# Projecting the values of all heads in a stage of their own, by one level of Strassen's algorithm, and reading them back per pair of heads

## The chip, the cores and the metric

The kernel runs on one core of a Trainium2 chip. The metric is the device time of one execution in microseconds (us). The kernel before takes 1388.06 us (median of 3 runs, 1387.71 to 1388.27). The profile is of one execution that took 1388.24 us, of which its span covers 1386.5 us.

The engines are named as in the profile: PE is the tensor engine (PEld its weight loads), DVE the vector engine, ACT the scalar engine, POOL the GpSimd engine, and SP the queue that issues every DMA. Each takes its instructions in a fixed order.

## The reference, cut to what matters

One decoder block over x of 512 tokens by 1024 features, in float32: a gated feed-forward layer with layer norm, then a mixer, a second layer norm, and a second feed-forward layer with layer norm. The part that the change touches is in the mixer.

```
proj = h @ w_in + b_in                       # h: 512 x 1024
q, k, v, g, glu_a, glu_b, gate_r, gate_c = split(proj)
q, k = rotary(q) * 128 ** -0.5, rotary(k)    # 8 heads of 128
v = v.reshape(8 heads of 256)                # v: 512 x 2048
scores = (q k^T) * decay_mask; r = scores @ v; r = per-head norm of r
ret_out = (silu(g) * r) @ w_ret_o
u = glu_a * sigmoid(glu_b); u = causal convolution of u, 31 taps per channel
```

## The kernel before, in words

Every float32 operand of a product is split into a high part, rounded to the type fp32r (a cast on ACT), and a low part, the difference (a subtraction on DVE). A product is three matmuls: high by high, high by low, low by high (`split`, L64 to L66, and `mm3`).

The two feed-forward layers use one level of Strassen's algorithm: seven products of half-size blocks in place of eight, with sums of blocks of the weights and of x made by DVE. In them x is the moving operand. The sums of x are made by the steps f1 to f4 of `strassen_x` (L127 in the profile).

The mixer starts when the first layer norm has written its result, as features by tokens, into `xh` and `xl` (high and low part). The end of the first layer already projects two units of weights of 1 MB, for q and k of head 0 and for channel block 0 of the convolution (`qk_glu`). Then four pairs of heads follow. For one pair:

- `v_half`, twice: the values of both heads, 512 tokens by 512 columns. A half is one 1 MB unit of weights and 48 matmuls with 512 columns, with x stationary (L701 to L703). The four results stay in PSUM until `v_out` adds the bias (L712) and splits them.
- `scores` of a head, `retain` (scores by values, the norm's statistics, `rn` on ACT at L780) and `gated` (eight transposes of `rn` at L789, multiplied by the gate).
- in between, units of 48 matmuls with 512 columns (`unit_proj`): q and k of the next head (`qk_proj`), the gate of a head (`g_unit`), a block of the convolution's input (`glu`).

The taps of the convolution run on DVE (L328), some after each unit (`TAPS_HEAD`, `TAPS_LATE`). In the mixer the order on each engine is set by a planner from the written order, by its own costs; in the feed-forward layers it is the written order (`manual_schedule`). A tile of a pool with one buffer is written again only when its last reader is done.

The names that the change and the steps of the prediction touch:

```
raw = wpool.tile([P, 2048], ..., bufs=2)     # one unit of weights, 1 MB, loaded by SP
whi, wlo: 4 buffers of [P, 1024]             # its high and low parts, two buffers per unit
def unit_proj(src, taps): load, split, 2 x 24 matmuls of 512 columns, then conv_some(taps)
```

Of the kernel before, what the change touches and what calls it, by code (L numbers as in the profile page):

```python
# [8 lines left out]
F32 = mybir.dt.float32  # L9
F32R = mybir.dt.float32r  # L10
# [5 lines left out]
P = 128  # L16
# [10 lines left out]
ALPHA = 2.0 ** 0.25  # L27
KR = 4
WARM = 18
TAPS_HEAD = 5  # L30
TAPS_LATE = 9
HS = S // 2
KH = KD // 2
N_STD = (2, 3)
# [18 lines left out]
def block_kernel(ctx, tc, ap, out):  # L53
# [7 lines left out]
    def bank():  # L61
        return psum.tile([P, S], F32, name="ps", tag="ps")
# [247 lines left out]
    def vcol(i):  # L310
        return vec[:, i:i + 1]
# [288 lines left out]
    def first_unit(h):  # L600
# [25 lines left out]
        nc.sync.dma_start(vec, ap["vec"])  # L626
        return [ps0]

    w_in = ap["w_in"]
    qk_glu = ffn(ap["w1gu"], ap["w1dn"], ap["x"], 0, scratch1, N_STD[0], first_unit, first_parts, (w_in[U_QK], w_in[U_L]))  # L630


    with ExitStack() as mix:
        mp = mix.enter_context(tc.tile_pool(name="mix", bufs=1))

        def spare_z(shape, dtype):
            return mp.tile(shape, dtype, name="z", tag="z", bufs=17)

        def tok(dtype=F32):
            return spare_z([P, S], dtype)  # L640

        def chan(dtype=F32):
            return mp.tile([P, S], dtype, name="cv", tag="cv", bufs=KD + 1)


        mp.tile([P, PAD + S], F32, name="up", bufs=5)
        mp.tile([P, 32], F32, name="gap")
        tok()
        cv = [chan() for _ in range(KD)]

        def gate_unit(i, pool, sc):
            ps = unit_proj(w_in[U_R + i], TAPS_LATE)
# [6 lines left out]
        with tc.tile_pool(name="heads", bufs=1) as hp_:  # L659
            cs = hp_.tile([P, 2, S], F32, name="cs")  # L660
            nc.sync.dma_start(cs, ap["cs"])

            def glu(i, ps=None):
                ps = ps or unit_proj(w_in[U_L + i], TAPS_HEAD)
                sgb = hp_.tile([P, S], F32, name="sgb", tag="t1", bufs=2)
                nc.scalar.activation(sgb, ps[0], AF.Sigmoid, bias=vcol(C_BIN + T_B + i))
                up = mp.tile([P, PAD + S], F32, name="up", bufs=5)
                nc.gpsimd.memset(up[:, :PAD], 0.0)
                nc.vector.scalar_tensor_tensor(up[:, PAD:], ps[1], vcol(C_BIN + T_A + i), sgb, op0=ALU.add, op1=ALU.mult)
                conv_todo.append(conv_taps(cv[i], up, i))  # L670

            def qk_proj(h, ps=None):

# [15 lines left out]
                    r.append((rh, rl))  # L689
                return r  # L690

            def v_half(hp, kk, vps):
                ws = load_unit(w_in[U_V + 2 * hp + kk])
                for k4 in range(4):
                    k = kk * 4 + k4
                    wh, wl = ws[k4 // 2]
                    csl = slice((k4 % 2) * 512, (k4 % 2) * 512 + 512)
                    for st in range(ST):
                        o = vps[st]
                        ssl = slice(st * P, (st + 1) * P)  # L700
                        mm(o, xh[:, k, ssl], wh[:, csl], start=(k == 0), stop=False)  # L701
                        mm(o, xh[:, k, ssl], wl[:, csl], start=False, stop=False)  # L702
                        mm(o, xl[:, k, ssl], wh[:, csl], start=False, stop=(k == KD - 1))  # L703

            def v_out(hp, vps):

                bv = hp_.tile([P, 512], F32, name="bv")
                nc.sync.dma_start(bv, ap["b_v"][hp:hp + 1, :].partition_broadcast(P))
# [85 lines left out]
            glus = iter(range(KD))  # L794
# [24 lines left out]

        gp = mix.enter_context(tc.tile_pool(name="gates", bufs=1))  # L820
# [85 lines left out]
    def split_parts(h):  # L906
        def parts(i, j):
            sl = (slice(None), slice(i * KH, (i + 1) * KH), slice(j * HS, (j + 1) * HS))
            return [(slice(0, KH), [p.bitcast(F32)[sl] for p in (xh, xl)])]

        return parts

    ffn(ap["w2gu"], ap["w2dn"], scratch2, 4, out, N_STD[1], lambda h: started, split_parts, ())


# [82 lines left out]
```

## Time and profile before

| | |
|---|---|
| median of 3 runs | 1388.06 us |
| profiled execution | 1388.24 us |
| its span | 1386.5 us |
| PE busy | 1371.2 us, 99% |
| DVE busy | 995.3 us, 72% |
| ACT busy | 597.5 us, 43% |
| the four pairs of heads | 383.6 to 772.2 us of the span |

A duration in the profile is from the start of an instruction to its end. Instructions on one engine overlap a little, so what an instruction costs in a queue is the distance from its start to the next start. A matmul of 512 columns is shown with 0.39 us but the next starts 0.23 us later.

### The profile page before, as it was taken

Reading aid. Unit: us, or ns where it says so; the run is one execution under the profiler, and the core shown is the slowest. Engines: PE = TensorE matmul, PEld = TensorE weight load, DVE = VectorE, ACT = ScalarE, POOL = GpSimd, SP = SyncE. Lnnn points to the kernel's source line nnn. Section 1 sums busy time; section 2 is a strip of 40 time slices with the busy share of each in tenths; the row PEclk is TensorE's granted clock in tenths of the full one; section 3 lists DMA queues with packets and bytes.
Section 4 is the critical chain, followed back from the end, with each engine's and each line's share of the span. In section 5 each row is a group of like instructions: output and inputs, shape, how many; then the busy total and the mean of one; then the engine's idle time right before and its main releaser. Section 6 shows DMA issues by size and latency. Waiting matters only on the chain.

```text
span 1386.5 us, 19271 instructions
## 1 busy us (share of the span) xinstructions
PE 1371.2 (99%) x7974; PEld 1215.4 (88%) x7974; DVE 995.3 (72%) x1422; ACT 597.5 (43%) x872; POOL 21.8 (2%) x36
## 2 busy tenths in 40 slices
PE   9899999999999999999999999999999999999997
PEld 7899999888988888888888888888889999998886
DVE  7878886435787787786787997555478988874336
ACT  5555554323434433444345522383234555544231
POOL 0000000000000000000000000000000000000000
PEclk9999999999999999999999999999999999999999
DMA  5323232524422232222221223232251323225221
GB/s 187 122 96 118 92 122 95 209 92 152 152 76 73 87 106 99 84 104 79 92 99 61 91 100 134 101 110 103 91 192 52 122 92 120 94 107 198 96 87 61
DMA packets 26006, 150.83 MB, mean 109 GB/s; under 512 B 2880, under 2 KB 3008, under 8 KB 10432
## 3 DMA queue, kind: packets, MB, share of 16 engines
q1 hardware_dynamic: 25920, 149.62, 30.2%
q8 instruction: 62, 1.02, 0.3%
q14 instruction: 24, 0.20, 0.0%
HBM read 143.32 MB, written 6.29 MB: 108 GB/s over the span
## 4 chain that ended last, share of the span: by engine, by line
PE 93%; DVE 4%; ACT 1%; DMA 0%; SPq 0%; issue 0%; POOL 0%; DVEq 0%; POOLq 0%
PE ps L201 26%; PE ps L437 19%; PE ps L295 13%; PE ps L296 13%; PE ps L294 13%; PE ps L701 2%; PE ps L702 2%; PE ps L703 2%; DVE wlo L158 1%; PE ps L789 1%; DMA h<-in_xT_dram 0%; DVE ln_y L406 0%; PE ps L418 0%; DVE st L165 0%; SPq L613 0%
## 5 line engine op out<-in xcount | busy, mean ns | idle before, releaser
L65 ACT CAST whi<-raw 128x1024 fp32r<-128x1024 f32 x156 | 162.5, 1051 | 270.4 <-PE ps L295 159.2
L66 DVE TENSOR_TENSOR wlo<-raw,whi 128x1024 fp32r<-128x1024 f32 x156 | 190.0, 1221 | 74.6 <-ACT whi L65 73.9
L294 PE MATMUL ps<-xh,whi 128*128 128x512 f32 x512 | 200.0, 391 | 0.0
L296 PE MATMUL ps<-xh,wlo 128*128 128x512 f32 x512 | 199.4, 389 | 0.2 <-DVE wlo L66 0.2
L295 PE MATMUL ps<-xl,whi 128*128 128x512 f32 x512 | 199.4, 389 | 0.0
L328 DVE SCALAR_TENSOR_TENSOR cv<-up,vec,cv 128x512 f32<-128x512 f32 x240 | 179.5, 748 | 4.2
L296 PEld LDWEIGHTS ps<-xh,wlo 128*128 128x128 f32 x512 | 96.1, 188 | 20.7 <-DVE wlo L66 0.6
L294 PEld LDWEIGHTS ps<-xh,whi 128*128 128x128 f32 x512 | 96.2, 188 | 19.4
L295 PEld LDWEIGHTS ps<-xl,whi 128*128 128x128 f32 x512 | 96.2, 188 | 19.3
L437 PE MATMUL ps<-whi,hh 128*128 128x512 f32 x320 | 100.0, 390 | 0.0
L437 PE MATMUL ps<-wlo,hh 128*128 128x512 f32 x320 | 99.9, 389 | 0.0
L437 PE MATMUL ps<-whi,hl 128*128 128x512 f32 x320 | 99.8, 389 | 0.0
L66 DVE TENSOR_TENSOR hl<-h,hh 128x512 fp32r<-128x512 f32 x40 | 27.3, 690 | 96.9 <-ACT hh L65 96.9
L201 PE MATMUL ps<-th,whi 128*128 128x256 f32 x312 | 88.5, 284 | 1.0 <-ACT z L209 1.0
L201 PE MATMUL ps<-xh,wlo 128*128 128x256 f32 x312 | 88.3, 283 | 0.0
L201 PE MATMUL ps<-xl,whi 128*128 128x256 f32 x312 | 88.3, 283 | 0.0
L201 PE MATMUL ps<-tl,whi 128*128 128x256 f32 x312 | 88.3, 283 | 0.0
L201 PE MATMUL ps<-xh,whi 128*128 128x256 f32 x312 | 88.3, 283 | 0.0
L201 PE MATMUL ps<-th,wlo 128*128 128x256 f32 x312 | 88.3, 283 | 0.0
L65 ACT CAST hh<-h 128x512 fp32r<-128x512 f32 x40 | 24.1, 622 | 115.2 <-PE ps L437 115.2
L437 PEld LDWEIGHTS ps<-whi,hl 128*128 128x128 f32 x320 | 60.1, 188 | 12.6
L437 PEld LDWEIGHTS ps<-wlo,hh 128*128 128x128 f32 x320 | 60.1, 188 | 12.5
(218 smaller groups left out, 3324.7 us busy)
## 6 DMA issues: line engine op xcount, KB each, us to landing
raw<-in_w_in_dram SPq DMA_DIRECT2D x40, 1024.0 KB, 4.8
raw<-in_w2gu_dram SPq DMA_DIRECT2D x22, 1024.0 KB, 4.8
raw<-in_w1gu_dram SPq DMA_DIRECT2D x21, 1024.0 KB, 4.8
raw<-in_w1dn_dram SPq DMA_DIRECT2D x11, 1024.0 KB, 4.9
raw<-in_w2dn_dram SPq DMA_DIRECT2D x11, 1024.0 KB, 4.8
raw<-in_w_ret_dram SPq DMA_DIRECT2D x8, 1024.0 KB, 4.8
ln_r<-scratch SPq DMA_DIRECT2D x8, 512.0 KB, 7.0
raw<-in_w_conv_dram SPq DMA_DIRECT2D x4, 1024.0 KB, 4.8
```

The costliest lines, as they stand in the source:

```text
L65: nc.scalar.copy(hi, src)
L66: nc.vector.tensor_tensor(lo, src, hi.bitcast(F32), op=ALU.subtract)
L158: return lambda: nc.vector.tensor_tensor(lo, src, hi.bitcast(F32), op=ALU.subtract)
L201: mm(ps, a[:, sl], c[:, k, :], start=(first and k == 0 and n == 0), stop=(k == KH - 1 and n == 2), skip_group_check=True)
L294: mm(ps, wh[wsl], xh[xsl], start=first, stop=False)
L295: mm(ps, wh[wsl], xl[xsl], start=False, stop=False)
L296: mm(ps, wl[wsl], xh[xsl], start=False, stop=last)
L328: op = nc.vector.scalar_tensor_tensor(c, up[:, t:t + S], vcol(C_CK + i * TAPS + t), c, op0=ALU.mult, op1=ALU.add)
L437: mm(acc[st][hf], x[:, sl], wx[:, hf * 512:(hf + 1) * 512], start=(k == 0 and x is ah and wi == 0), stop=(k == nk - 1 and x is al),)
L701: mm(o, xh[:, k, ssl], wh[:, csl], start=(k == 0), stop=False)
L702: mm(o, xh[:, k, ssl], wl[:, csl], start=False, stop=False)
L703: mm(o, xl[:, k, ssl], wh[:, csl], start=False, stop=(k == KD - 1))
```

## The change

The values of all eight heads are computed before the first pair, in a stage whose order is the written one. The weights of the values (1024 by 2048) are taken in two halves of 1024 columns (u is 0 or 1). Each half is one product of two by two blocks by Strassen's algorithm: seven products of 24 matmuls with 512 columns, x stationary, where before the eight units of weights took 48 matmuls each. DVE makes the sums of the weights (`add`) and of x (`f1` to `f4`), takes partial results with the bias out of PSUM (`take`), and adds the last parts (`give`); `give` also stores 128 by 512 values to a scratch tensor in memory. In the pairs, `v_in` loads four such tiles and splits them.

The early units are now block 0 of the convolution first and then q and k of head 0. The second block of the convolution is projected just before the first pair, and the remaining blocks one place earlier than before, so that in the last pair `g_unit(b)` takes the place of `glu`. `TAPS_HEAD` goes from 5 to 6 and `TAPS_LATE` from 9 to 10, and the taps after `v_half` are gone. The diff, cut to its core:

```
-TAPS_HEAD = 5
-TAPS_LATE = 9
+TAPS_HEAD = 6
+TAPS_LATE = 10
-    qk_glu = ffn(..., first_unit, first_parts, (w_in[U_QK], w_in[U_L]))
+    glu_qk = ffn(..., first_unit, first_parts, (w_in[U_L], w_in[U_QK]))
+        values = dram.tile([H // 2, ST, P, 512], F32, name="values")
+        with tc.tile_pool(name="values", bufs=1, reuse_waits="tile") as vp, tc.manual_schedule():
+            ...
+            def load(u, name):
+                ...
+                nc.sync.dma_start(raw[u, name], w_in[U_V + 2 * (2 * u + i) + j])
+            def add(u, name, a, b):
+                ...
+                for c in range(2):
+                    sl = slice(c * 1024, (c + 1) * 1024)
+                    nc.vector.tensor_tensor(sums[u, name][:, sl], a[:, sl], b[:, sl], op=ALU.add)
+            def block(u, name):
+                ...
+                for c in range(2):
+                    hi = wpool.tile([P, 1024], F32R, name="whi", tag="whi")
+                    lo = wpool.tile([P, 1024], F32R, name="wlo", tag="wlo")
+                    split(hi, lo, src[:, c * 1024:(c + 1) * 1024])
+            def product(ps, w, x, first):
+                h_, l_ = x
+                for k in range(KH):
+                    wh, wl = w[k // 2]
+                    csl = slice((k % 2) * 512, (k % 2) * 512 + 512)
+                    for st in range(2):
+                        ssl = slice(st * P, (st + 1) * P)
+                        for n, (a, c) in enumerate(((h_, wh), (h_, wl), (l_, wh))):
+                            mm(ps[st], a[:, k, ssl], c[:, csl], start=..., stop=...)
+            def take(u, name, ps, row, op):
+                t = vp.tile([P, 2, 512], F32, name=name)
+                for st in range(2):
+                    nc.vector.tensor_tensor(t[:, st], ps[st], bv[u][row], op=op)
+                return t
+            def give(u, row, half, a, b, op):
+                for st in range(2):
+                    o = vp.tile([P, 512], F32, name="vo", bufs=5)
+                    nc.vector.tensor_tensor(o, a[st], b[st], op=op)
+                    nc.sync.dma_start(values[2 * u + row, 2 * half + st], o)
+            def biases(u):
+                bv[u] = [vp.tile([P, 512], F32, name=f"bv{row}") for row in range(2)]
+                for row in range(2):
+                    nc.sync.dma_start(bv[u][row], ...)
+            for name in ("a11", "a12", "a21", "a22"):
+                load(0, name)
+            biases(0)
+            block(0, "a11")
+            block(0, "a12")
+            add(0, "s3", "a11", "a21")
+            add(0, "s1", "a21", "a22")
+            do("f3 hi3 f1 lo3")
+            ups = [glu(0, vp, glu_qk[0])]
+            product(z, ready[0, "a11"], xs["b11"], True)
+            do("f2 hi2")
+            block(0, "s3")
+            do("lo2")
+            z1 = take(0, "z1", z, 0, ALU.add)
+            product(w, ready[0, "a12"], xs["b21"], True)
+            add(0, "s2", "s1", "a11")
+            load(1, "a11")
+            block(0, "s2")
+            give(0, 0, 0, two(z1), w, ALU.add)
+            product(y, ready[0, "s3"], xs["t3"], True)
+            do("f4 hi4 lo4")
+            block(0, "a22")
+            load(1, "a21")
+            y1 = take(0, "y1", y, 1, ALU.add)
+            product(z, ready[0, "s2"], xs["t2"], False)
+            do("hi1 lo1")
+            block(0, "s1")
+            z2 = take(0, "z2", z, 1, ALU.subtract)
+            product(y, ready[0, "a22"], xs["t4"], False)
+            ...
+            product(z, ready[0, "s4"], xs["b22"], False)
+            block(1, "s3")
+            give(0, 0, 1, z, bv[0][:1] * 2, ALU.add)
+            biases(1)
+            z1 = take(1, "z1", w, 0, ALU.add)
+
+            product(y, ready[1, "s3"], xs["t3"], True)
+            add(1, "s1", "a21", "a22")
+            add(1, "s2", "s1", "a11")
+            block(1, "s2")
+            y1 = take(1, "y1", y, 1, ALU.add)
+            product(w, ready[1, "s2"], xs["t2"], False)
+            ...
-            def v_half(hp, kk, vps):
-                ...
-            def v_out(hp, vps):
+            def v_in(hp):
                 v = []
                 for st in range(ST):
-                    vf = hp_.tile([P, 512], F32, name="vf", tag="t1", bufs=2)
-                    nc.vector.tensor_tensor(vf, vps[st], bv, op=ALU.add)
+                    vf = hp_.tile([P, 512], F32, name="vf", bufs=2)
+                    nc.sync.dma_start(vf, values[hp, st])
-            qk = qk_proj(0, qk_glu[0])
-            glu(next(glus), qk_glu[1])
+            qk = qk_proj(0, glu_qk[1])
+            glu_next()
             for hp in range(H // 2):
                 a, b = 2 * hp, 2 * hp + 1
-                vps = [bank() for _ in range(ST)]
-                v_half(hp, 0, vps)
-                conv_some(TAPS_HEAD)
                 pa = scores(a, qk)
-                v_half(hp, 1, vps)
-                conv_some(TAPS_HEAD)
-                v = v_out(hp, vps)
+                v = v_in(hp)
                 qk = qk_proj(b)
                 ra = retain(a, pa, v)
                 ga = g_unit(a)
                 gated(a, ra, ga)
                 pb = scores(b, qk)
-                glu(next(glus))
+                gb = None if glu_next() else g_unit(b)
                 rb = retain(b, pb, v)
-                gb = g_unit(b)
+                gb = gb or g_unit(b)
                 gated(b, rb, gb)
                 if hp < H // 2 - 1:
                     qk = qk_proj(b + 1)
-                    glu(next(glus))
+                    glu_next()
```

What this does to the order is shown at three places. The first is SP's queue from the end of the first feed-forward layer into the new stage, as a difference of the two kernels (L410 and L408 are the stores of the layer norm's result, L680 the loads of the values' weights, L730 the two biases).

```order
 L87 DMA raw<-in_w_in_dram 128x2048 x2
+L410 DMA scratch_80<-ln_y 128x1024 x3
+L408 DMA scratch_80<-ln_y 128x512 x2
+L680 DMA a_3964<-in_w_in_dram 128x2048
+L680 DMA raw<-in_w_in_dram 128x2048
+L680 DMA a_3968<-in_w_in_dram 128x2048
+L680 DMA raw<-in_w_in_dram 128x2048
+L730 DMA bv_3972<-in_b_v_dram 128x512
+L730 DMA bv_3973<-in_b_v_dram 128x512
```

All four loads of the first half of the values stand behind the last stores of the layer norm; before, two units of weights stood ahead of its first store. Further down the same queue the biases of the second half (bv_4337, bv_4338) stand behind the stores of `give`:

```order
+L720 DMA values<-vo 128x512 x4
+L730 DMA bv_4337<-in_b_v_dram 128x512
+L730 DMA bv_4338<-in_b_v_dram 128x512
+L720 DMA values<-vo 128x512 x2
+L75 DMA raw<-in_w_in_dram 128x2048
```

The last two of these four stores wait for the `give` that is the last reader of the old biases. The second place is ACT at the end of the stage in the changed kernel (whi is the split of weights, rs and rh belong to q and k of head 0, vh to the values read back, sgb to block 1 of the convolution):

```order
253 L65 CAST whi<-raw 128x1024 x4
254 L847 ACTIVATE rs<-ps,vec 64x512
255 L848 ACTIVATE rs<-ps,vec 64x512
256 L847 ACTIVATE rs<-ps,vec 64x512
257 L848 ACTIVATE rs<-ps,vec 64x512
258 L65 CAST whi<-raw 128x1024 x2
259 L65 CAST vh<-vf 128x512 x2
260 L65 CAST rh<-rc 128x512
261 L650 ACTIVATE sgb<-ps,vec 128x512
262 L65 CAST rh<-rc 128x512
```

In the kernel before the same casts of q and k stand ahead of the split of weights:

```order
238 L681 ACTIVATE rs<-ps,vec 64x512
239 L682 ACTIVATE rs<-ps,vec 64x512
240 L681 ACTIVATE rs<-ps,vec 64x512
241 L65 CAST rh<-rc 128x512
242 L682 ACTIVATE rs<-ps,vec 64x512
243 L666 ACT_TABLE_LOAD
244 L666 ACTIVATE sgb<-ps,vec 128x512
245 L65 CAST rh<-rc 128x512
246 L65 CAST whi<-raw 128x1024 x2
```

The third place is PE at the end of the last pair, first in the kernel before and then in the changed one (vh,pl are the last matmuls of `retain`, ident,rn the transposes of `gated`, xh,whi a unit of weights).

```order
3977 L296 MATMUL ps<-vh,pl 128x256
3978 L294 MATMUL ps<-xh,whi 128x512
3979 L295 MATMUL ps<-xl,whi 128x512
3980 L296 MATMUL ps<-xh,wlo 128x512
3981 L294 MATMUL ps<-xh,whi 128x512
```

```order
3976 L295 MATMUL ps<-vl,ph 128x256
3977 L296 MATMUL ps<-vh,pl 128x256
3978 L940 MATMUL ps<-ident,rn 128x128 x8
3979 L294 MATMUL ps<-xh,whi 128x512
3980 L295 MATMUL ps<-xl,whi 128x512
```

Before, the unit of `g_unit(b)` stands between the two; in the changed kernel it stands ahead of `retain`, in the place that `glu` had.

## Rows read from the trace of the kernel before

**Rows 1.** The page: span and busy time; section 4, the chain's share.

```profile
span 1386.5 us, 19271 instructions
PE 1371.2 (99%) x7974; PEld 1215.4 (88%) x7974; DVE 995.3 (72%) x1422; ACT 597.5 (43%) x872; POOL 21.8 (2%) x36
...
PE 93%; DVE 4%; ACT 1%; DMA 0%; SPq 0%; issue 0%; POOL 0%; DVEq 0%; POOLq 0%
```

**Rows 2.** Stretches: start:end, length, busy us (count) per engine, PEclk, DMA, GB/s.

```profile
345.00:383.60 38.60, 38.04 (x275) 35.70 (x274) 30.01 (x52) 16.33 (x25) 2.65 (x4) 1.00 0.41 153
583.50:683.50 100.00, 100.00 (x486) 84.59 (x485) 78.09 (x124) 43.24 (x59) 2.93 (x3) 1.00 0.26 93
785.00:883.00 98.00, 98.00 (x440) 81.28 (x439) 75.71 (x95) 25.90 (x31) 0.00 (x0) 1.00 0.33 118
```

**Rows 3.** Timeline of PE: start, duration, engine, line; first half of values.

```profile
383.62 0.40 PE L701 MATMUL ps<-whi,xh 128*128 128x512 f32 x1
...
394.52 0.39 PE L294 MATMUL ps<-rh 128*128 128x512 f32 x1
```

**Rows 4.** Groups by form: line, operation, shapes, count, busy us, mean ns.

```profile
L701 PE MATMUL ps<-whi,xh 128*128 128x512 f32 x128 | 50.0, 391 | 0.0
L65 ACT CAST whi<-raw 128x1024 fp32r<-128x1024 f32 x156 | 162.5, 1051 | 270.4 <-PE ps L295 159.2 <-PE ps L703 40.3 <-issue 32.2
```

**Rows 5.** Timeline of DVE, second feed-forward layer: sums and low parts.

```profile
1042.80 1.22 DVE L127 TENSOR_TENSOR st<-xh,xl 128x1024 f32<-128x1024 f32 x1
1044.05 1.23 DVE L127 TENSOR_TENSOR st<-st,xh 128x1024 f32<-128x1024 f32 x1
1045.31 1.23 DVE L127 TENSOR_TENSOR st<-st,xl 128x1024 f32<-128x1024 f32 x1
1046.46 1.22 DVE L158 TENSOR_TENSOR wlo<-raw,whi 128x1024 fp32r<-128x1024 f32 x1
```

**Rows 6.** Timeline of DVE: end of layer norm; sums with bias out of PSUM.

```profile
360.77 1.22 DVE L66 TENSOR_TENSOR wlo<-raw,whi 128x1024 fp32r<-128x1024 f32 x1
362.50 1.21 DVE L66 TENSOR_TENSOR wlo<-raw,whi 128x1024 fp32r<-128x1024 f32 x1
365.68 1.41 DVE L406 SCALAR_TENSOR_TENSOR ln_y<-ln_r,ln_i,ln_b 128x512 f32<-128x512 f32 x2
369.88 1.28 DVE L66 TENSOR_TENSOR xl<-ps,xh 128x512 fp32r<-128x512 f32 x2
508.07 1.28 DVE L712 TENSOR_TENSOR vf<-ps,bv 128x512 f32<-128x512 f32 x2
```

**Rows 7.** SP's timeline; issues with KB and us to landing; rate at the start.

```profile
366.46 0.98 SPq L408 DMA_DIRECT2D scratch<-ln_y  x2
...
raw<-in_w_in_dram SPq DMA_DIRECT2D x40, 1024.0 KB, 4.8
...
12.00:14.00 2.00, 2.00 (x11) 1.65 (x10) 2.00 (x4) 1.90 (x4) 0.00 (x0) 1.00 1.06 410
```

**Rows 8.** Tile bv: DMA to landing; the mask's and the stores' landing.

```profile
DMA to landing us min/median/max: 3.2/3.5/4.0
...
DMA to landing us min/median/max: 2.4/3.8/4.1
...
scratch<-ln_y SPq DMA_DIRECT2D x4, 256.0 KB, 4.4
```

**Rows 9.** Timeline at the end of the last pair: PE, DVE, ACT, PE.

```profile
749.63 0.28 PE L296 MATMUL ps<-vh,pl 128*128 128x256 f32 x1
...
754.27 0.16 DVE L777 SCALAR_TENSOR_TENSOR gnm<-gmv,grs 128x4 f32<-128x4 f32 x1 [0.90 <-POOL grs L776]
...
754.53 1.94 ACT L780 ACTIVATE rn<-ps,gnm,grs 128x256 f32<-128x256 f32 x4 [7.29 <-DVE gnm L777]
...
760.66 1.03 PE L789 MATMUL ps<-ident,rn 128*128 128x128 f32 x8
```

**Rows 10.** PE's first transposes, the same shape in the chain, the clock there.

```profile
1.36 4.10 PE L592 MATMUL ps<-ident 128*128 128x128 f32 x18 [1.36 <-POOL ident masks.py:199]
...
432.87 0.87 PE ps L789 x8
...
2.00:3.00 1.00, 1.00 (x7) 1.00 (x6) 0.00 (x0) 0.01 (x1) 0.00 (x0) 1.00 0.72 182
```

**Rows 11.** Groups of DVE by form in one pair, 583.5 to 683.5: the taps.

```profile
L328 DVE SCALAR_TENSOR_TENSOR cv<-up,vec,cv 128x512 f32<-128x512 f32 x40 | 29.9, 747 | 0.6
```

More of the change, by code (lines that the diff above doesn't have):

```diff
@@ L627, in first_unit, with split_parts, parts @@
         return [ps0]
+    def split_parts(h):
+        def parts(i, j):
+            sl = (slice(None), slice(i * KH, (i + 1) * KH), slice(j * HS, (j + 1) * HS))
+            return [(slice(0, KH), [p.bitcast(F32)[sl] for p in (xh, xl)])]
+        return parts
     w_in = ap["w_in"]
-    qk_glu = ffn(ap["w1gu"], ap["w1dn"], ap["x"], 0, scratch1, N_STD[0], first_unit, first_parts, (w_in[U_QK], w_in[U_L]))
+    glu_qk = ffn(ap["w1gu"], ap["w1dn"], ap["x"], 0, scratch1, N_STD[0], first_unit, first_parts, (w_in[U_L], w_in[U_QK]))
@@ new lines, in block_kernel, with two, do @@
+        values = dram.tile([H // 2, ST, P, 512], F32, name="values")
+        with tc.tile_pool(name="values", bufs=1, reuse_waits="tile") as vp, tc.manual_schedule():
+            for name in ("z1", "y1", "z2"):
+                vp.tile([P, 2, 512], F32, name=name)
+            vp.tile([P, 512], F32, name="vo", bufs=5)
+            for name in ("bv0", "bv1"):
+                vp.tile([P, 512], F32, name=name)
+            vp.tile([P, KH, HS], F32, name="st", bufs=3)
+            for name in ("th", "tl"):
+                vp.tile([P, KH, HS], F32R, name=name, bufs=4)
+            vp.tile([P, 2048], F32, name="sum", bufs=2)
+            vp.tile([P, S], F32, name="sgb", tag="t1", bufs=2)
+            vp.tile([P, 2048], F32, name="gap1")
+            xs, x_steps = strassen_x(vp, split_parts(None))
+            raw, sums, ready = {}, {}, {}
+            def load(u, name):
+                i, j = int(name[1]) - 1, int(name[2]) - 1
+                if name in ("a11", "a21"):
+                    raw[u, name] = vp.tile([P, 2048], F32, name=name)
+                else:
+                    raw[u, name] = wpool.tile([P, 2048], F32, name="raw", tag="raw", bufs=2)
+                nc.sync.dma_start(raw[u, name], w_in[U_V + 2 * (2 * u + i) + j])
+            def add(u, name, a, b):
+                sums[u, name] = vp.tile([P, 2048], F32, name="sum", bufs=2)
+                a, b = ((sums if n[0] == "s" else raw)[u, n] for n in (a, b))
+                for c in range(2):
+                    sl = slice(c * 1024, (c + 1) * 1024)
+                    nc.vector.tensor_tensor(sums[u, name][:, sl], a[:, sl], b[:, sl], op=ALU.add)
+            def block(u, name):
+                src = (sums if name[0] == "s" else raw)[u, name]
+                ready[u, name] = []
+                for c in range(2):
+                    hi = wpool.tile([P, 1024], F32R, name="whi", tag="whi")
+                    lo = wpool.tile([P, 1024], F32R, name="wlo", tag="wlo")
+                    split(hi, lo, src[:, c * 1024:(c + 1) * 1024])
+                    ready[u, name].append((hi, lo))
+            def product(ps, w, x, first):
[6 more added lines that the diff above has]
+                        for n, (a, c) in enumerate(((h_, wh), (h_, wl), (l_, wh))):
+                            mm(ps[st], a[:, k, ssl], c[:, csl], start=(first and k == 0 and n == 0),
+                               stop=(k == KH - 1 and n == 2), skip_group_check=True)
+            def take(u, name, ps, row, op):
[8 more added lines that the diff above has]
+                    nc.sync.dma_start(values[2 * u + row, 2 * half + st], o)
+            def two(t):
+                return t[:, 0], t[:, 1]
+            bv = {}
+            def biases(u):
+                bv[u] = [vp.tile([P, 512], F32, name=f"bv{row}") for row in range(2)]
+                for row in range(2):
+                    nc.sync.dma_start(bv[u][row], ap["b_v"][2 * u + row:2 * u + row + 1, :].partition_broadcast(P))
+            def do(names):
+                for name in names.split():
+                    x_steps[name]()
+            for name in ("a11", "a12", "a21", "a22"):
[7 more added lines that the diff above has]
+            ups = [glu(0, vp, glu_qk[0])]
+            z, w = ([bank() for _ in range(2)] for _ in range(2))
+            y = [bank() for _ in range(2)]
+            product(z, ready[0, "a11"], xs["b11"], True)
[18 more added lines that the diff above has]
+            product(y, ready[0, "a22"], xs["t4"], False)
+            block(1, "a11")
+            give(0, 1, 0, y, two(z2), ALU.subtract)
+            product(z, ready[0, "s1"], xs["t1"], False)
+            add(0, "s4", "s2", "a12")
+            load(1, "a12")
+            load(1, "a22")
+            give(0, 1, 1, two(y1), z, ALU.subtract)
+            product(w, ready[1, "a11"], xs["b11"], True)
+            block(0, "s4")
+            add(1, "s3", "a11", "a21")
+            product(z, ready[0, "s4"], xs["b22"], False)
[9 more added lines that the diff above has]
+            product(w, ready[1, "s2"], xs["t2"], False)
+            block(1, "a12")
+            z2 = take(1, "z2", w, 1, ALU.subtract)
+            product(z, ready[1, "a12"], xs["b21"], True)
+            block(1, "s1")
+            give(1, 0, 0, two(z1), z, ALU.add)
+            product(w, ready[1, "s1"], xs["t1"], False)
+            block(1, "a22")
+            give(1, 1, 1, two(y1), w, ALU.subtract)
+            product(y, ready[1, "a22"], xs["t4"], False)
+            add(1, "s4", "s2", "a12")
+            block(1, "s4")
+            give(1, 1, 0, y, two(z2), ALU.subtract)
+            product(w, ready[1, "s4"], xs["b22"], False)
+            give(1, 0, 1, w, bv[1][:1] * 2, ALU.add)
@@ L636, in spare_z @@
+        mz = mix.enter_context(tc.tile_pool(name="mixz", bufs=1, reuse_waits="tile"))
         def spare_z(shape, dtype):
-            return mp.tile(shape, dtype, name="z", tag="z", bufs=17)
+            return mz.tile(shape, dtype, name="z", tag="z", bufs=17)
         def tok(dtype=F32):
@@ L661, in block_kernel, with glu_next @@
             nc.sync.dma_start(cs, ap["cs"])
[L663 to L670, printed above, removed]
+            def glu_next():
+                if len(ups) == KD:
+                    return False
+                ups.append(glu(len(ups), hp_))
+                conv_todo.append(conv_taps(cv[len(ups) - 1], ups[-1], len(ups) - 1))
+                return True
             def qk_proj(h, ps=None):
@@ L903, in block_kernel @@
         started = token_proj(KD, lambda k: m[k], unit_rows(ap["w_out"]), ln, ((ap["w2gu"][0], ap["w2gu"][1]), spare_z))
[L906 to L911, printed above, removed]
     ffn(ap["w2gu"], ap["w2dn"], scratch2, 4, out, N_STD[1], lambda h: started, split_parts, ())
```

29 lines of the change are left out of this document (12 added, 17 removed).

## The prediction

> **What bounds the kernel now.** I read the page's span and engine table first, then its chain, then stretches by engine, then timelines at the places where the change cuts in. PE is busy 1371.2 of 1386.5 us and holds 93% of the chain [rows 1]. In a pair of heads PE is busy 100.00 of 100.00 us beside DVE with 78.09 and ACT with 43.24, so no wait of PE is left in the pairs; in the stretch ahead of them (end of the first layer, layer norm, first units) PE misses 0.56 of 38.60 us [rows 2]. So matmul time removed counts in full, and so does each new wait of PE. The sum is made against the profiled execution: 1386.5 us of span and 1.74 around it, 1388.24; the median of the runs is 1388.06, 0.18 less.
>
> **PE's matmuls.** A half of the values is 48 matmuls in 394.52 − 383.62 = 10.90 us, 227.1 ns each [rows 3]. (The 391 ns of the group [rows 4] is from start to end and overlaps the next.) Before there are eight units of 48, 384 matmuls; after, 2 x 7 products of 24, 336. A product is 5.45 us. 48 matmuls go: **−10.9 us**.
>
> **The first products wait for DVE, +7.6.** DVE must make sums, splits of sums and sums of x that did not exist before, and PE has only 5.45 us per product. A 128 by 1024 sum starts 1.14 to 1.15 us after the last one where it reads nothing from it, and 1.25 to 1.26 where it does [rows 5]; a cast on ACT is 1.05 [rows 4]. DVE is free for this at 371.1: the low parts of x start at 369.88 [rows 6]. The loads of the four blocks stand behind the layer norm's last stores, at 366.46 with two units of weights already served [rows 7]; of those units two splits of 1.13 leave DVE ahead of the norm [rows 6], so I start the loads at 364.8. At 410 GB/s a megabyte takes 2.6 us, and a single load lands after 4.8 [rows 7]: the blocks are there at 370.3, 372.9, 375.5 and 378.1.
>
> DVE's written order then gives: low parts of a11 by 373.7 and a12 by 376.2, sums s3 by 378.5 and s1 by 380.8, f3 by 384.45, f1 by 388.1, lo3 and the convolution's `up` by 389.9, f2 by 392.4, low parts of s3 by 396.8, lo2, z1 by 401.4 with s2's first sums, s2's low parts by 404.9 with `give`, f4 by 407.3, lo4 409.65, a22's low parts 411.9, first half of y1 412.6. PE starts the stage at 383.2 and runs z and w until 394.1. Product y on s3 waits for its first low part at 395.65 (its first matmul, high by high, hides the rest of the step): 1.35 lost. Product z on s2 waits for 402.6: 1.45. Product y on a22 may not write its bank until `y1` has read it, at 412.6 instead of 407.8: 4.85. Sum 7.6. Bounds: if the loads and ACT never bind, DVE's instructions alone, 37.7 us from 371.1, end at 408.8 where PE without waits is at 405.0: 3.8. If the four loads come one after the other at 4.8, a22 lands at 384, 5.6 later: 13.2. I take 7.6, as the start row shows four loads at once at 410 GB/s.
>
> **The biases of the second half, +5.9.** Each `bv` has one buffer; its load for the second half stands on SP behind the stores of the `give` that reads it last. With E the end of product z on s4, that `give` is done at E + 0.75 (its first sum goes beside the last matmuls of the other bank, its second takes 0.6), the load is issued at E + 1.1 behind a store, and it lands 3.5 us later, E + 4.6 (3.2 to 4.0 [rows 8]). Behind the waiting `z1` on DVE stand s1's and s2's sums and the first low part of s2: 1.2 + 2.3 + 1.14 + ACT's cast 1.05 + 1.14 is E + 11.5. PE has meanwhile only product y on s3, 5.45 us, and its next product hides 0.2 more: 5.9. Bounds: landing 3.2 and no cast in the chain, 4.8; landing 4.1 as the mask does [rows 8] and dependent pitch throughout, 7.5. In the rest of the half DVE has fewer than five long instructions per product and PE does not wait.
>
> **From the stage into the pairs, +5.8.** PE's last work before `scores` of head 0 is the unit of convolution block 1 (10.9 us). On ACT the split of the next unit's weights stands ahead of `vh` and of `rh` (the second order above); the cast needs a buffer that PE's last high-part matmul in the unit frees, at G. Then cast 1.05, two `vh` of 0.6, `rh` is out at G + 3.0, `rl` 0.65 later, `sgb`, second `rh` G + 4.95, its `rl` about G + 6.15. The first matmuls of `scores` hide 0.4: 5.8. Bounds: without the `vh` in the chain 4.5; with the load of `vf` (256 KB, 4.4 us as the stores of that size [rows 8]) late behind the last `give`, 9.
>
> **The end of the last pair, +7.0.** Before, the last `retain` ends at 749.87, `gnm` is at 754.27 behind POOL's root, ACT's four `rn` run from 754.53 to 756.47, and the transposes come at 760.66, behind a unit of weights that covers the chain [rows 9]. After, this unit stands ahead of `retain` and the transposes directly behind it (the third order). The chain of 756.47 − 749.87 = 6.6 is bare; 0.2 of semaphores, less 0.8 as transposes begin at the second `rn`: 6.0 at least. DVE reaches the statistics later, behind two taps of 0.67 (40 taps in a pair, 747 ns each [rows 11]; that pitch is theirs less the overlap) or one low part: I take 1.0 more. High end: a tap, low part and tap, 8.5.
>
> **PE after a pause, +4.2.** The four waits are 4.9, 5.9, 5.8 and 7.0 us, where before has none above 1.4 behind the start. What the trace shows of PE after idling is its start: the first 18 transposes take 4.10 us, 228 ns each, and eight of the same shape later 0.87, 109 ns; the granted clock of that first stretch reads 1.00 of 2.4 GHz all the same [rows 10]. So 2.1 us are lost per event, for a reason the column doesn't tell. Bounds: no event, 0; all four, 8.4. I take two. The Trainium skill ("TensorE: Matmul & The Clock Gate", "HAM oscillation — how this bites in real kernels") says that a PE which idles between bursts falls back to half its clock and must warm up anew each time. By it all four count and the sum is 4.2 higher; the row agrees in pace and not in the column.
>
> **Edits at nothing.** Per pair DVE loses four low parts of 1.2 us, four sums of 0.7 and four taps of 0.75, 10.6 in all: 67.5 against PE's 100 − 96 x 0.227 = 78.2. So the pairs stay PE's; without this cover see the third rival. The rotary chain of q and k (7.6 us from the unit's end to `rl`) is now covered by one unit of 10.9 instead of two. In the gates after the pairs DVE has 22 us left in 98 [rows 2]; one more tap in each of nine units is 6. The 16 loads of values land in 4.4 us and are due a unit later, except at the edge above. The 16 stores and the casts (28 splits where 16 were) lie on SP and on ACT, which is under half busy.
>
> **Sum.** −10.9 + 7.6 + 5.9 + 5.8 + 7.0 + 4.2 = +19.6: 1388.2 + 19.6 = **1407.8 us**. All low bounds: −10.9 + 3.8 + 4.8 + 4.5 + 6.0 + 0 = +8.2, 1396.4. All high: −10.9 + 13.2 + 7.5 + 9 + 8.5 + 8.4 = +35.7, 1423.9.
>
> **Rivals.**
> - PE is slow after all four waits and after the short ones of 1.4 too: 2.1 x 6 = 12.6 in place of 4.2, 1416.2. For it: the first transposes; against it: the clock column.
> - Not slower: DVE's wide instructions in the stage at half the length of the rows, 0.6 instead of 1.14 us per 128 by 1024. Then the first products never wait, the biases cost 5.9 − 2.9 = 3.0, the edge 4.5, the end 5.0, no pause of length is left that slows PE: −10.9 + 12.5 = +1.6, 1389.8. It decides where the waits sum to less than 10.9 + 2.8 = 13.7. For it: the operands are all in SBUF; against it: the sums of the second layer have the same shapes and show 1.22 [rows 5].
> - The pairs become DVE's. Stretches with much DVE work are 78% busy [rows 2]; if DVE can't be fuller, a pair takes 67.5/0.78 = 86.5 us, 8.3 over 78.2. Half of that in four pairs is +16.6: 1424. Against it: 22 us of slack in the pair before cost nothing.
> - The change doesn't do what it says: values would be formed twice, or the pairs keep their units. The order of PE excludes it.
>
> **How the numbers follow.** Forecast 0.62, its own range 1396 to 1416; slow PE everywhere 0.14; DVE-bound pairs 0.06; halved DVE 0.12, of it 0.06 faster (with one wait fewer) and 0.05 the same; what I don't see 0.06, of it 0.02 faster and 0.02 the same. About 2.8 us, 0.2%, is what a measurement here tells from no change. Faster 0.08, same 0.07, slower 0.85. 1394 to 1420 holds the forecast, the slow PE and a little of the rest, 8 in 10.
>
> **What would show it.** PE's timeline in the new stage: waits on low parts and `y1` in the first half, and one of about 6 us ahead of the product on s2 of the second half, with DVE's `z1` released by the DMA of `bv`. Before the first `scores`: PE waits for `rl`, and ACT's `rh` stands behind two casts of weights. At the last pair: the transposes released by ACT's `rn`, some 7 us after `retain`. Matmuls of 512 columns further apart than 227 ns right behind these waits. PE's share of the pairs stays at 100%. I am wrong where these waits are absent or sum to less than 13.7, or where PE waits for DVE inside the pairs.

## The result and the profile after

The changed kernel takes 1412.65 us (median of 4 runs, 1410.21 to 1413.11), the kernel before 1388.16 beside it: a ratio of 1.0173 [1.0156, 1.0191], 24.5 us slower. The forecast was 1407.8, 19.6 slower, in a range of 1394 to 1420. The profiled execution spans 1411.3 us; from here times are of that execution, 24.8 us longer than the profiled one of before.

From the page of the profile: the span, the busy time, and the shares of the chain of work that ended last ([rows 1] for before):

```profile
span 1411.3 us, 19332 instructions
...
PE 1371.6 (97%) x7926; PEld 1212.5 (86%) x7926; DVE 1050.3 (74%) x1476; ACT 608.9 (43%) x886; POOL 21.2 (1%) x36
...
PE 83%; DVE 10%; DMA 3%; issue 2%; ACT 2%; POOL 0%; SPq 0%; DVEq 0%; ACTq 0%; POOLq 0%
```

PE has 48 instructions fewer, as counted, and yet its busy time has not fallen: part of its matmuls ran slower. Its share of the chain fell from 93% to 83%. What PE waited for (line, releaser: us in total, times, longest us):

```profile
PE ps L294 <- issue: 7.1, 1, 7.1
PE ps L706 <- ACT whi L65: 5.7, 2, 5.5
PE ps L940 <- ACT rn L931: 5.4, 1, 5.4
PE ps L706 <- DVE y L713: 4.5, 1, 4.5
PE ps L706 <- DVE wlo L66: 2.0, 3, 0.8
```

These are the four places of the prediction. L706 is the values' products: 4.48 for `y1` and 0.27, 0.76 and 0.76 ahead of it are the first half, 6.3 in all; 5.45 and 0.47 are the second half, 5.9. L294 is the first `scores` (7.05), L940 the last transposes (5.44). Stretches right behind the four waits, and 100 us inside the pairs (start:end, length, busy us and count per engine, PEclk, DMA, GB/s; [rows 2] for before):

```profile
413.06:417.00 3.94, 3.94 (x10) 3.10 (x11) 3.94 (x5) 0.45 (x1) 0.00 (x0) 0.57 0.02 4
447.59:455.00 7.41, 6.94 (x17) 5.17 (x18) 5.80 (x6) 3.99 (x4) 0.00 (x0) 0.56 0.01 2
496.49:502.00 5.51, 5.51 (x17) 4.67 (x18) 5.51 (x11) 2.20 (x5) 0.00 (x0) 0.51 0.45 125
783.78:789.00 5.22, 5.21 (x17) 4.01 (x18) 5.08 (x9) 2.76 (x6) 0.00 (x0) 0.54 0.00 0
595.00:695.00 100.00, 100.00 (x493) 84.87 (x493) 86.29 (x146) 49.60 (x71) 4.14 (x5) 1.00 0.30 103
```

The granted clock falls to half, 1.2 instead of 2.4 GHz, late in each of these waits or at its end. Otherwise it is at its full level, but for the last 5 us of the span, where PE has no work left; the kernel before has the same fall at its end. Length times what is missing of the clock is 1.7 + 3.3 + 2.7 + 2.4, 10.0 before rounding; of it 0.2 lies in a wait, so 9.8 us are lost to slow matmuls. In the pairs PE is never idle, as forecast. PE's timeline shows wait and pace (start, duration; in brackets the idle time and what ended it):

```profile
408.19 0.39 PE L706 MATMUL ps<-whi,tl 128*128 128x512 f32 x1
413.06 0.70 PE L706 MATMUL ps<-whi,th 128*128 128x512 f32 x1 [4.48 <-DVE y L713]
413.56 0.63 PE L706 MATMUL ps<-wlo,th 128*128 128x512 f32 x1
413.99 0.63 PE L706 MATMUL ps<-whi,tl 128*128 128x512 f32 x1
414.42 0.63 PE L706 MATMUL ps<-whi,th 128*128 128x512 f32 x1
```

From start to start it is 0.43 us where [rows 3] has 0.227. The sum: −10.9 + 6.3 + 5.9 + 7.05 + 5.44 + 9.8 = +23.6 of 24.8; 1.2 us, in small pieces, I did not follow.

The biases, on DVE: `z1` waits for the load, the sums s1 and s2 stand behind it, and with ACT's cast PE starts at 447.59.

```profile
441.69 1.29 DVE L713 TENSOR_TENSOR z<-ps,bv 128x512 f32<-128x512 f32 x2 [4.26 <-DMA bv<-in_b_v_dram]
442.90 2.35 DVE L687 TENSOR_TENSOR sum<-a,raw 128x1024 f32<-128x1024 f32 x2
445.17 2.35 DVE L687 TENSOR_TENSOR sum<-sum,a 128x1024 f32<-128x1024 f32 x2
```

Ahead of the first `scores`, on ACT: `rs` could not start before the last values were stored, and `rh` came behind the casts of the next weights and two `vh`. In this chain the first `vh` waited 1.16 us for the load of `vf`, and the first `rh` 0.36 us for `rc` on DVE.

```profile
485.05 0.69 ACT L847 ACTIVATE rs<-ps,vec 64x512 f32<-64x512 f32 x1 [5.40 <-DMA values<-vo]
...
487.85 1.05 ACT L65 CAST whi<-raw 128x1024 fp32r<-128x1024 f32 x1
489.58 1.05 ACT L65 CAST whi<-raw 128x1024 fp32r<-128x1024 f32 x1 [0.69 <-PE ps L296]
491.79 1.22 ACT L65 CAST vh<-vf 128x512 fp32r<-128x512 f32 x2 [1.16 <-DMA vf<-values]
493.37 0.62 ACT L65 CAST rh<-rc 128x512 fp32r<-128x512 f32 x1 [0.36 <-DVE rc L851]
...
495.78 0.62 ACT L65 CAST rh<-rc 128x512 fp32r<-128x512 f32 x1
```

The last pair, PE's transposes behind `retain` (they answer to [rows 9]):

```profile
778.06 0.28 PE L296 MATMUL ps<-vh,pl 128*128 128x256 f32 x1
783.78 2.06 PE L940 MATMUL ps<-ident,rn 128*128 128x128 f32 x8 [5.44 <-ACT rn L931]
```

The eight transposes take 2.06 us from the first start to the last end; at the full clock they took 1.03 [rows 9].

### The profile page after: what moved, and what is told of

It reads as the page before. It is cut to its first block, busy times and chain, and to the rows that moved or that the text cites. A ratio compares the mean times of both kernels' runs of the same rounds, so it can differ in the third digit from the quotient of the medians.

```text
span 1411.3 us, 19332 instructions
## 1 busy us (share of the span) xinstructions
PE 1371.6 (97%) x7926; PEld 1212.5 (86%) x7926; DVE 1050.3 (74%) x1476; ACT 608.9 (43%) x886; POOL 21.2 (1%) x36
## 4 chain that ended last, share of the span: by engine, by line
PE 83%; DVE 10%; DMA 3%; issue 2%; ACT 2%; POOL 0%; SPq 0%; DVEq 0%; ACTq 0%; POOLq 0%
PE ps L201 26%; PE ps L437 15%; PE ps L294 13%; PE ps L295 13%; PE ps L296 12%; PE ps L706 4%; DVE wlo L66 1%; DMA raw<-in_w_in_dram 1%; DVE st L127 1%; DMA h<-in_xT_dram 1%; DMA raw<-in_w2gu_dram 1%; DVE ln_y L406 1%; DVE sum L687 1%; DVE wlo L158 1%; PE ps L940 1%
## 5 line engine op out<-in xcount | busy, mean ns | idle before, releaser
L65 ACT CAST whi<-raw 128x1024 fp32r<-128x1024 f32 x148 | 153.9, 1051 | 225.7 <-PE ps L295 157.2
L66 DVE TENSOR_TENSOR wlo<-raw,whi 128x1024 fp32r<-128x1024 f32 x148 | 179.7, 1221 | 63.9 <-ACT whi L65 63.4
L294 PE MATMUL ps<-xh,whi 128*128 128x512 f32 x512 | 201.5, 394 | 0.0
L294 PEld LDWEIGHTS ps<-xh,whi 128*128 128x128 f32 x512 | 96.9, 189 | 19.6
```

The costliest lines, as they stand in the source:

```text
L65: nc.scalar.copy(hi, src)
L66: nc.vector.tensor_tensor(lo, src, hi.bitcast(F32), op=ALU.subtract)
L294: mm(ps, wh[wsl], xh[xsl], start=first, stop=False)
```

## The experiments

All but the last three are read against the changed kernel's 1412.65; each run's ratio is to the kernel before, measured on the same chip (1388.3 to 1388.4). Runs of one such kernel spread by 1 to 5 us, so a wait is read from the profile and the time is its check.

**The clock: fill_wait.** 20 matmuls whose result is not used stand in the last wait.

```
 gb = gb or g_unit(b)
+if hp == H // 2 - 1:
+    idle = bank()
+    for n in range(20):
+        mm(idle, xh[:, n % KD, :P], xh[:, n % KD, :], start=(n == 0), stop=(n == 19))
 gated(b, rb, gb)
```

> 20 matmuls of 512 columns on x whose result is not used stand in PE's wait between the last retain and its transposes (4.5 of 5.4 us); all else is as in the changed kernel. Theory (the pause makes the clock fall): the transposes come at the same time as before, the granted clock stays at 1.00 and the 4.9 us at half the clock are gone: 2 to 2.5 us less, 1410 to 1411. Rival (the clock falls for another reason): half the clock all the same and no gain, 1412 to 1413.

1411.45, 1.0166 [1.0152, 1.0179]. PE's timeline and the stretch behind:

```profile
778.78 4.72 PE L962 MATMUL ps<-xh 128*128 128x512 f32 x20
784.39 0.44 PE L940 MATMUL ps<-ident,rn 128*128 128x128 f32 x2 [0.88 <-ACT rn L931]
```

```profile
784.39:789.00 4.61, 4.61 (x24) 3.80 (x25) 4.47 (x8) 2.16 (x5) 0.00 (x0) 1.00 0.00 0
```

The transposes come no sooner, but the clock stays at 1.00: the pause makes it fall. The median's gain of 1.2 us is within the runs' spread, so the 2.4 us stand on the profile. Part of that spread may be the clock's own: behind the same wait of 4.5 us for `y1` the fall cost 1.7 us in the changed kernel's profiled execution and 3.4 us in this one.

**The biases: bias_early and bias_spare.** Both load the second half's biases early; in the first their tiles move others by 4 KB, in the second they take a spare tile's place.

```
 load(1, "a21")
+biases(1)                    # bias_early: right behind biases(0)
 ...
 give(0, 0, 1, z, bv[0][:1] * 2, ALU.add)
-biases(1)
```

> Both halves' biases have buffers of their own and are loaded at the start of the stage; nothing else differs from the changed kernel (1412.65 us). Theory (the second half's first take waits for the load of the biases behind the stores): the take no longer waits 4.26 us for the load, PE's wait of 5.45 ahead of the product on s2 of the second half falls to about 1.9 (DVE's chain of sums and splits remains), and PE's clock does not fall behind it, worth about 3 more: 1405 to 1407 us. Rival (DVE's own work is late in any case and the load only shows up last): the wait falls by less than 1 us, 1411 to 1413.

> The changed kernel with the biases of the second half in tiles at the place of a spare tile, so that no other tile moves (in bias_early tiles had moved by 4 KB and the first sum of x waited 2 us for PE), and loaded behind a21 of the second half. Theory: PE's wait ahead of the product on s2 of the second half falls from 5.9 to about 1.6 as in bias_early, the first half is as in the changed kernel, and no 6 us at half the clock follow: 1405 to 1407 us. Rival (what bias_early gained came from elsewhere): over 1410.

1408.69, 1.0149 [1.0136, 1.0163], 1.7 us above its expected range, and 1406.69, 1.0133 [1.0119, 1.0147], within it. In both the wait is 1.1 + 0.76 (bias_spare, PE):

```profile
442.82 0.51 PE L708 MATMUL ps<-whi,th 128*128 128x512 f32 x1 [1.09 <-ACT whi L65]
444.08 0.71 PE L708 MATMUL ps<-wlo,th 128*128 128x512 f32 x1 [0.76 <-DVE wlo L66]
```

So 4.1 of the 5.9 were the load. In bias_early the moved tiles made the first sum of x wait 1.96 us for PE, and a wait of 2.79 with a fall of the clock came in the first half, which hid part of the gain. In bias_spare the clock fell for some 3 us behind the short waits all the same.

**The first half: first_order and first_pool.** Only ACT's and DVE's order; then s1 on POOL.

```
-do("f2 hi2"); block(0, "s3"); do("lo2")
+high(0, "s3"); do("f2 hi2"); low(0, "s3", 0); low(0, "s3", 1); do("lo2")
 ...
-give(0, 0, 0, ...)                         # now behind the low parts of s1
-do("f4 hi4 lo4"); block(0, "a22"); y1 = take(0, "y1", ...)
+high(0, "a22"); do("f4 hi4"); y1 = take(0, "y1", ...); low(0, "a22", 0); do("lo4"); low(0, "a22", 1)
```

> In the first half of the values ACT's and DVE's order alone is changed: the casts of s3 ahead of the one of t2, those of a22 ahead of the one of t4, y1 taken ahead of a22's low parts, the first give behind those of s1. Theory (DVE's order and two waits of DVE for ACT, 2.06 and 1.11 us, make PE late): PE's waits in the first half, 0.5 + 1.0 + 1.5 + 4.5, fall to about 3 in all and the clock does not fall there (1.8): 1406 to 1409 us. Rival (DVE's sum of work is the bound, whatever the order): the wait moves to a later product and 1411 to 1413 stays.

> As first_order, and the sum s1 = a21 + a22 of the first half (2 x 128 by 1024) is made by POOL, which is idle there. Theory: DVE is free 2.3 us sooner and POOL's sum is done before s2 needs it at about 397: another 1 to 2 us less than first_order. Rival: the sum on POOL takes over 8 us each or slows DVE's instructions beside it: no gain or a loss against first_order.

1405.89, 1.0132 [1.0118, 1.0146], and 1406.93, 1.0133 [1.0118, 1.0149]. With the order alone PE's waits in the first half are 0.15, 0.25, 0.77 and 0.63, and the clock stays at its full level there: the order of ACT and DVE was the cause, not DVE's sum of work. POOL brought nothing. POOL's and then DVE's timeline of first_pool:

```profile
379.27 6.19 POOL L688 TENSOR_TENSOR sum<-a,raw 128x1024 f32<-128x1024 f32 x2 [15.90 <-DMA bv<-in_b_v_dram]
```

```profile
379.79 3.43 DVE L127 TENSOR_TENSOR st<-xh,xl 128x1024 f32<-128x1024 f32 x1
383.25 3.30 DVE L127 TENSOR_TENSOR st<-st,xh 128x1024 f32<-128x1024 f32 x1
386.58 1.22 DVE L127 TENSOR_TENSOR st<-st,xl 128x1024 f32<-128x1024 f32 x1
```

POOL takes 3.1 us for a half here, and the two sums of DVE beside it take 3.4 and 3.3 instead of 1.22: DVE loses 4.3 us to be spared 2.3. The Trainium skill ("SBUF — State Buffer", "SBUF: two separate sides") says that GpSimd and a DVE instruction with two SBUF inputs hold one port in turn, each for its whole instruction. These rows agree: 3.4 and 3.3 us beside POOL, 1.22 right behind.

**Ahead of the first scores: heads_by_tile and edge_order.**

```
-with tc.tile_pool(name="heads", bufs=1) as hp_:
+with tc.tile_pool(name="heads", bufs=1, reuse_waits="tile") as hp_:
 # edge_order besides: cs loaded by nc.gpsimd; the unit of block 1 and the rotary of head 0 in
 # written order; casts of v_in(0) and qk_proj(1) behind the rotary's last rh
```

> The pool of the heads' tiles waits tile by tile for the memory of the values' stage, not for the whole stage's end; the order on every engine is the same. Theory M (q and k of head 0 start late because their memory is free only when the last stores of values have landed): rs starts at about 479 and not 485, and PE's wait of 7.05 us ahead of the first scores falls to 3 or less, 1406 to 1409 us. Theory O (the prediction's: ACT's order binds, rh behind the cast of the next unit's weights and two vh): rs is early, but rh still comes behind that cast; the wait falls only to 5.5 to 6: 1411 to 1412.5.

> The heads' memory by tile, cs loaded by POOL's queue instead of SP's, and on ACT and DVE the rotary step of q and k of head 0 ahead of the taps, of the split of the values read back and of the next units' weights. Theory (three things in a row make rl late: memory, the load of cs on SP and ACT's order): rl is done before PE has finished the unit of block 1; the wait of 7.05 us ahead of the first scores falls below 1, and the 5 us at half the clock behind it go: 1403 to 1406 us. Rival (the values' way through memory binds: the last stores and the four loads make retain late instead): a wait of 3 or more comes ahead of retain, 1408 to 1412.

1411.12, 1.0163 [1.015, 1.0177], and 1409.71, 1.0157 [1.0143, 1.017]. In heads_by_tile `rs` starts at 480.44 instead of 485.05, but the wait is still 4.92: neither theory alone. ACT and DVE of heads_by_tile:

```profile
490.01 1.04 ACT L65 CAST whi<-raw 128x1024 fp32r<-128x1024 f32 x1 [4.38 <-PE ps L295]
490.97 1.13 ACT L65 CAST vh<-vf 128x512 fp32r<-128x512 f32 x2
492.05 0.62 ACT L65 CAST rh<-rc 128x512 fp32r<-128x512 f32 x1
```

```profile
489.40 0.75 DVE L849 SCALAR_TENSOR_TENSOR rc<-ps,vec,cs 128x512 f32<-128x512 f32 x1 [1.85 <-DMA cs<-in_cs_dram]
```

The memory made up 1 to 2 us (the other kernels that leave this place alone wait 6.0 to 7.2 there). What is left is ACT's order, as forecast, and the load of `cs`, for which `rc` now waits 1.85; no run takes these two apart. edge_order takes both away: 2.16 left (expected under 1). all_four below has the same 2.16 and shows its cause on DVE, `up` waiting for the end of the unit ahead of the second `rc`:

```profile
476.20 0.75 DVE L659 SCALAR_TENSOR_TENSOR up<-ps,vec,sgb 128x512 f32<-128x512 f32 x1 [4.83 <-PE ps L302]
476.87 0.68 DVE L881 TENSOR_TENSOR rc<-rc,rs 128x512 f32<-128x512 f32 x1
```

The median of edge_order gained only 2.9 of the 7 to 10 expected. Its profile has a fall of the clock of 3 us behind waits of 1.08 and 0.76 near 396, where the changed kernel has none, and one of 3 us behind the 2.16. So shortening a wait to 2.16 us did not do away with the fall behind it.

**The last pair: gate_last and gate_half.** The first unit of the gates ahead of the transposes; then cut in two halves around them.

```
+gate0 = unit_proj(w_in[U_R], TAPS_LATE)    # gate_last; gate_half: 24 matmuls here,
 gated(b, rb, gb)
+                                           # gate_half: the other 24 here
```

> In the last pair the first unit of the gates is projected between retain and the transposes; its two sigmoids stay where they were. Theory (the chain of the norm is bare because no unit stands there): PE's wait of 5.44 us ahead of the transposes goes, and the 4.9 us at half the clock behind it (2.5 lost); the first products of the retention's output come sooner and wait about 2 us for their first cast and low part: 1405 to 1408 us. Rival (the clock falls on its own, not because of the wait): 1407 to 1409 with a stretch at half the clock near the place all the same.

> The changed kernel with the first unit of the gates cut in two, 24 matmuls ahead of the last transposes and 24 behind them. Theory (5.45 us of matmuls cover the bare part of the norm's chain, and the other half covers the casts that gate_last left bare): the waits of 5.44 and of gate_last's 4.24 are both under 1 us and the clock stays: 1404 to 1406 us; with a wait of about 1.5 and a clock's fall on the next unit's low part, as in all_four, 1407 to 1409. Rival (the casts' memory keeps the wait of over 4): 1410 or more.

1411.18, 1.0165 [1.0151, 1.0179], and 1407.88, 1.0141 [1.0127, 1.0155]. gate_last has no wait ahead of the transposes, but one behind them:

```profile
PE ps L294 <- ACT zh L65: 4.2, 1, 4.2
```

I had expected 2: behind the last `gated` nothing covered ACT, which waited for DVE's last `z` and then ran two sigmoids ahead of the casts `zh`. The clock falls behind this wait too (1.7 us lost), which leaves little of the gain. With the unit cut, both waits are gone and 1.5 is left at the next unit's low part. The time is that of the second case that was expected, though the profile shows no fall of the clock there. In all_four below the same waits stand at this place, and there the clock falls (PE, gate_half and then all_four; the durations show the pace):

```profile
809.33 0.50 PE L296 MATMUL ps<-zh,wlo 128*128 128x512 f32 x1 [1.52 <-DVE wlo L66]
```

```profile
793.29 0.80 PE L302 MATMUL ps<-zh,wlo 128*128 128x512 f32 x1 [1.52 <-DVE wlo L72]
```

**All together: all_four, all_mended, all_mended2.**

> first_order and edge_order together, the biases of the second half loaded early into tiles of their own (at the place of a spare tile, so that nothing else moves), s1 and z1 of the second half taken before the last product of the first, and the first unit of the gates cut in two: 24 matmuls ahead of the last transposes and 24 behind them. Theory (the change costs its four waits and the clock behind them, and saves 10.9 us of matmuls): with waits of 3 to 6 us left and no fall of the clock 1381 to 1385 us, faster than the kernel before (1388.2). Rival (DVE or ACT are full in the stage, and waits come back elsewhere): 1392 or more.

> all_four with three more changes of order: on DVE the up of block 1 stands behind the rotary's low parts (in all_four DVE waited 4.83 us for it and rh came 2.16 late); s2 of the second half is summed before z1 is taken; and no taps follow the split unit of the gates, one more follows each unit of the retention's output. Theory: the waits of 2.2 + 0.5, 1.5 and 1.5 us and the two stretches at half the clock (1.5 and 1.6 lost) go: 1381 to 1384 us, faster than the kernel before (1388.4). Rival (something outside these waits costs what all_four lacked): 1387 or more.

> all_mended with the order of DVE changed at two places: in the second half z1 is taken ahead of the sums s1 and s2, and s2's low parts stand ahead of the last give of the first half (in all_mended s2's low part came 2.36 us late behind them); and the first two low parts of the values read back stand ahead of the up of block 1 (in all_mended DVE waited 2.66 us for the unit's end there, and retain waited 0.99 for ph and 1.82 for vl). Theory: these 5 us of waits shrink to 1 or 2: 1385 to 1387 us, a little faster than the kernel before. Rival: DVE is full at both places (14.7 of 15 us busy around the first), so the waits move to the next product or to retain's other inputs, and 1388 to 1390 stays.

| | time, us | ratio to before |
|---|---|---|
| all_four | 1390.84 | 1.0021 [1.0012, 1.003] |
| all_mended | 1389.58 | 1.0009 [0.9999, 1.0018] |
| all_mended2 | 1388.19 | 0.9998 [0.9989, 1.0007] |

Their edits of order are told in the expectations, and the short form of the last two is:

```
+z1 = take(1, "z1", ...); add(1, "s1", ...); add(1, "s2", ...); block(1, "s2")   # all_mended2: ahead of
 give(0, 0, 1, ...)                                                             # the last give
 # up of block 1 behind the rotary's low parts (all_mended), behind the first two vl (all_mended2)
-    conv_some(TAPS_LATE)          # behind the split unit of the gates
-TAPS_LATE = 10
+TAPS_LATE = 11
```

24.5 us of loss are gone, and no version is faster than the kernel before; each came out above its expected range, by 6, 6 and 1 us. In all_mended2 the waits are short, but PE (timeline, then the stretch) shows where the rest goes:

```profile
479.25 0.50 PE L300 MATMUL ps<-xh,whi 128*128 128x512 f32 x1 [1.18 <-ACT whi L67]
...
480.46 0.38 PE L302 MATMUL ps<-vh,pl 128*128 128x256 f32 x1 [0.47 <-DVE pl L72]
```

```profile
481.00:488.00 7.00, 6.63 (x21) 5.21 (x20) 7.00 (x15) 0.60 (x2) 0.00 (x0) 0.51 0.39 105
```

Two waits of 1.18 and 0.47 were enough for the clock to fall, 3.2 us lost; all_mended, with single waits of 2.37, 0.99 and 1.82, shows no fall before the end in its profiled execution, which took 1387.8. Its runs take 1387.6 to 1390.6, and only this one has a trace, so whether the clock fell in the slower ones is open. By the places of PE's first and last instructions of a kind in all_mended2, the stage loses 3.5 us, the pairs 6.1 (the 3.2 among them) and the last pair's end 1.0: 10.6 of the 10.9 that the matmuls save.

## Why the prediction was right

The direction and the mechanism were right: the 48 matmuls are saved, and four waits that were not there cost more. That the total is only 5 us off is in part luck, as the terms below show. By its own steps:

- Matmuls, −10.9: PE has 48 fewer instructions at the pace of [rows 3]; the units taken out of the pairs left no waits, PE 100.00 of 100.00, and DVE's 86.29 beside it is the 67.5 of 78.2 that was forecast.
- First products, 7.6 forecast, 6.3 measured. The place of each wait was right (`y1` 4.85 forecast, 4.48). first_order shows what the step did not say: it was the order of DVE and ACT, not the amount of DVE's work, which the lower bound of 3.8 took for unavoidable; 1.8 is left with another order.
- Biases, 5.9 and 5.9; without the load 1.9 are left, from DVE's chain that was in the sum.
- The edge, 5.8 forecast, 7.05: ACT's order as told, but the late case of the bound (up to 9) took part. The load of `vf`, named for it, did hold ACT for 1.16 us; what the step did not see is the memory behind it. The heads' pool waits for the whole stage, so `rs`, `vf` and `cs` all start behind the landing of the last stores, near 485. With the memory by tile the wait for `vf` is gone, and 1 to 2 us of PE's wait with it.
- The end, 7.0 forecast, 5.44, below its low bound of 6.0. From the end of `retain` (778.06 + 0.28) to the first `rn` (783.17) it is 4.8 us, before 4.6 (749.63 + 0.28 to 754.53 [rows 9]): DVE came hardly later, where I had added 1.0; and the transposes begin behind the first of the four `rn`, at 783.78, where the bound had only 0.8 of their 1.94 us covered.
- PE after a pause, 4.2 forecast for two events, 9.8 measured for four of 1.7 to 3.1. This is the term that was mis-sized: both the count and the price. The row of the first transposes was a poor witness for the column: the clock column does show the later falls (0.50). fill_wait shows the cause. The Trainium skill ("TensorE: Matmul & The Clock Gate", "HAM oscillation — how this bites in real kernels") says that a PE which idles between bursts falls back to half its clock; the trace agrees, at all four waits. By it all four count, to which I gave the lesser chance.

The errors of the waits nearly cancel (26.3 forecast, 24.7 measured), and that is luck: two came out lower by 1.3 and 1.6, one higher by 1.25. So the miss of 5 us in the total is the clock's. Of the rivals, PE slow behind every wait came closest (1416.2). Four of its six events are there; behind the two short waits that it also counts (1.56 us near 37, which the prediction took for 1.4, and 1.36 near 45) the clock column stays at 1.00. The halved DVE is excluded by the 2.35 us for two sums, and DVE-bound pairs by PE's 100.00 beside DVE's 86.29.

## What to carry to other kernels

Fewer matmuls on an engine that is 99% busy pay only where their operands arrive without a pause: price each new wait with the slow stretch behind it, here another 1.7 to 3.1 us for waits of 4.5 to 7. Look for the wait at the seams of the new stage (tiles with one buffer, a pool that waits for the whole pool before it, the last iteration that lost its covering unit), as the four seams took 24.7 us and all four places were read from the order beforehand. Mending them, by order and by where tiles lie, gave back what was lost, but not the gain: of the 11 us of matmuls saved, 10.6 came back at or near the same seams, in short waits and one fall of the clock. In the stretch of all_mended2 shown above, DVE, which makes the sums and splits, was busy 7.00 of 7.00 us; that it is the limit at every one of these places is not shown.

## What the hardware showed that was not expected

- DVE's sums of two SBUF tiles took 3.4 and 3.3 us instead of 1.22 beside POOL's sum of two SBUF tiles (3.1 us a half).
- The clock's fall isn't told by the length of one wait: none behind 2.37 us in the profiled execution of all_mended, one behind 1.18 and 0.47 close together in all_mended2, and behind the same waits, the last of 1.52 us, one in all_four and none in gate_half. Nor is its price: 1.7 and 3.4 us behind the same wait of 4.5. What decides is left open.
- The first transposes at half pace with a clock column of 1.00 [rows 10] stay unexplained; in the falls seen here the column reads 0.50.
